# A hybrid encoder layer: gated sums ahead of the bank's sigmoid, first rows of the up half loaded twice, the last norm moved forward, and the down half's first pair made in memory that comes free earlier

## The chip, the cores and the metric

The kernel runs on one core of a Trainium2 chip. The metric is the device time of one execution in microseconds (us). Each time is a median over runs; the profile is of one execution of its own. Engines are named as the profile names them: PE multiplies matrices (PEld loads its weights), DVE is the vector engine, ACT the scalar engine, POOL the general one, SP only starts DMA transfers. Each engine works through its own instructions in order and waits on semaphores for the others.

## The reference

One layer of an encoder, on two sequences of 512 tokens with a model width of 1024, all in float32. The kernel handles the two sequences together (`s` = 0 and 1).

```python
h = rms_norm(x, ln1)
proj = h @ w_in
q, k, v, u, g_att, g_ssm = jnp.split(proj, IN_SPLITS, axis=-1)
...
y_att = windowed_attention(q, k, v, sink, bias, band_mask(seq_len))
y_ssm = s5_branch(u, ...)          # gelu(y) * sigmoid(gelu(y) @ w_glu + b_glu)
mixed = jax.nn.sigmoid(g_att) * y_att + jax.nn.sigmoid(g_ssm) * y_ssm
x = x + mixed @ w_out
h2 = rms_norm(x, ln2)
return x + jnp.square(jax.nn.relu(h2 @ w_up)) @ w_down
```

The inner width of the last line, the squared-ReLU MLP, is 4096.

## The kernel before, in words

Precision is kept by splitting each float32 operand into a high part (a cast to fp32r, on ACT) and a low part (the operand less the high part, a subtract on DVE). One product of two split tiles is three matmuls (`mm3`): high by high (L115), high by low (L116), low by high (L117). So wherever new operands are made, PE waits for a cast on ACT first and for a subtract on DVE second. Order on each engine is set by a scheduler that follows the program's order and its dependencies; where tiles share memory, a later tile waits until the earlier one's last reader is done.

The parts of the program that matter here, in order of time:

**Attention's last division (around 690 to 715 us).** `Divide.invert` makes `rsum` on DVE (L1106); `Divide.turn` transposes it on PE (L1111), copies it to `row` on ACT, sends it to DRAM (`rs_scr<-row`) and fetches it back spread out (`fac`), the DMAs on POOL's queue; `Divide.multiply` multiplies by it on POOL (L1124). Beside that PE computes `ahead`, the first column of the GLU product (`Column.multiply`, L758), in pieces of so many matmuls.

**The GLU (about 700 to 775).** For each column m = 1 to 7 and each sequence s: 24 matmuls into a bank, then `bank_out` (a sigmoid on ACT, L1415, tile `gl`), then `late()`, which is the `mix` of the bank before: two DVE instructions (L1421, L1422, tile `z`), a cast (L1424) and a subtract (L1425) that write the split result into `mixT[s]`. For s = 0 `gate_in` adds a sigmoid of 1024 and two DVE products (L1409 to L1411). The result of column 0 is written by `first_evac` (L1433, L1434). `mixT[0]` lies in `slot_c`, `mixT[1]` in `slot_d`; the tile `row` and others of the attention held memory now under `slot_c`.

**Output projection and second norm (to about 885).** `mixT` times `w_out` plus x, row tile by row tile (class `Rows`): `half` multiplies, `add` and `square` add x and sum the squares, three POOL instructions make `rs`, `norm` makes `rn_xn` (DVE L1524), `turn` transposes it on PE (L1532), and `first_rows`, `old_rows`, `sums_a`, `sums_b` and `sums_c` make the split operands of the MLP.

**The up half (to 1181).** A Strassen-like scheme (Winograd's form): seven products in place of eight on 2 x 2 blocks. One block of `w_up`, r = 0 to 15, gives products p1, p2, p6, p7, p5, p3, p4 in this order, of 12 matmuls each; the right operands B11, B21 (in the memory of `mixT[0]`), T1, B22 (in that of `mixT[1]`), T2, T3, T4 stay. `first_parts` splits the weights of the first two blocks into `f_0` and `f_1` (L1471 cast, L1472 subtract); in `parts` the same is `u_hi` (L1663) and `u_lo` (L1664). Squared-ReLU sums go to DRAM as `a_scr` (tags a22, a21, a12, t1 to t4).

**The down half (from 1181).** `product_d(n)` runs over eight pairs of blocks: it loads `d_a` from `a_scr` (L1797) and `k` from `w_down` (L1800), splits both (L1810 casts, L1811 subtracts: `a_hi`, `a_lo`, `b_hi`, `b_lo`) and makes 24 matmuls into four banks. The order of the seven products is 1, 5, 6, 3, 7, 2, 4.

## Time and profile before

| | us |
|---|---|
| median of 3 runs (lowest, highest) | 1501.79 (1499.71, 1502.31) |
| profiled execution, time | 1500.58 |
| its span | 1498.8 |
| mean granted clock of PE | 0.995 |
| PE busy | 1462.7 (98%) |
| DVE busy | 1095.9 (73%) |
| ACT busy | 764.9 (51%) |
| POOL busy | 168.9 (11%) |

The span is the time between the first and the last instruction of the profiled execution. Matmuls overlap, so one of 512 columns shows 0.39 us though the next starts 0.23 us after it. A row of the timeline has the start, the time, engine, line, operation, the tiles written and read, the count, and in brackets the idle time ahead of it with what ended it.

### The profile page before, as it was taken

Reading aid. Unit: us, or ns where it says so; the run is one execution under the profiler, and the core shown is the slowest. Engines: PE = TensorE matmul, PEld = TensorE weight load, DVE = VectorE, ACT = ScalarE, POOL = GpSimd, SP = SyncE. Lnnn points to the kernel's source line nnn. Section 1 sums busy time; section 2 is a strip of 40 time slices with the busy share of each in tenths; the row PEclk is TensorE's granted clock in tenths of the full one; section 3 lists DMA queues with packets and bytes.
Section 4 is the critical chain, followed back from the end, with each engine's and each line's share of the span. In section 5 each row is a group of like instructions: output and inputs, shape, how many; then the busy total and the mean of one; then the engine's idle time right before and its main releaser. Section 6 shows DMA issues by size and latency. Waiting matters only on the chain.

```text
span 1498.8 us, 22161 instructions
## 1 busy us (share of the span) xinstructions
PE 1462.7 (98%) x8070; PEld 1253.3 (84%) x8070; DVE 1095.9 (73%) x1835; ACT 764.9 (51%) x1366; POOL 168.9 (11%) x270
## 2 busy tenths in 40 slices
PE   6999999999999999999999999999999899999999
PEld 5888888889998888987889978888888688888787
DVE  8799979964637888887874689777776597575653
ACT  6588952234427777786433355555555343433332
POOL 4011120000313333342001000000000000000000
PEclk9999999999999999999999999999999999999999
DMA  8355566459832323147853134444443974454431
GB/s 298 109 174 171 178 218 231 132 181 291 263 101 61 98 65 109 46 149 246 271 198 107 71 121 161 153 148 149 155 155 127 349 268 128 153 183 154 125 121 64
DMA packets 128809, 242.86 MB, mean 162 GB/s; under 512 B 16011, under 2 KB 59275, under 8 KB 128700
## 3 DMA queue, kind: packets, MB, share of 16 engines
q1 hardware_dynamic: 104252, 185.82, 39.1%
q10 hardware_dynamic: 21888, 46.15, 8.1%
q0 software_dynamic: 2560, 9.48, 1.9%
q8 instruction: 64, 1.05, 0.3%
q14 instruction: 45, 0.37, 0.1%
HBM read 172.16 MB, written 81.82 MB: 169 GB/s over the span
## 4 chain that ended last, share of the span: by engine, by line
PE 83%; DVE 7%; ACT 3%; DMA 3%; issue 2%; POOL 1%; SPq 0%; DVEq 0%; ACTq 0%; POOLq 0%
PE bank L116 13%; PE bank L117 13%; PE bank L115 13%; PE acc L146 11%; PE acc L729 7%; PE acc L115 3%; PE acc L117 3%; PE acc L116 3%; PE sps L609 2%; PE po L1085 2%; PE sps L865 2%; PE sps L1053 2%; PE tps L1069 2%; PE lag L624 1%; DVE p L1057 1%
## 5 line engine op out<-in xcount | busy, mean ns | idle before, releaser
L115 PE MATMUL bank<-b_hi,a_hi 128*128 128x512 f32 x448 | 174.2, 392 | 3.9 <-ACT b_hi L1810 3.9
L116 PE MATMUL bank<-b_lo,a_hi 128*128 128x512 f32 x448 | 175.5, 392 | 2.1 <-DVE b_lo L1811 2.0
L117 PE MATMUL bank<-b_hi,a_lo 128*128 128x512 f32 x448 | 175.1, 391 | 0.0
L729 PE MATMUL acc<-w_hi,hT 128*128 128x256 f32 x768 | 165.0, 291 | 0.0
L146 PE MATMUL acc<-hT,c_hi 128*128 128x512 f32 x512 | 161.0, 394 | 0.0
L1810 ACT CAST a_hi<-d_a 128x1024 fp32r<-128x1024 f32 x56 | 59.0, 1054 | 182.0 <-PE bank L116 178.1
L1811 DVE TENSOR_TENSOR a_lo<-d_a,a_hi 128x1024 fp32r<-128x1024 f32 x56 | 68.4, 1223 | 107.1 <-ACT a_hi L1810 105.3
L729 PEld LDWEIGHTS acc<-w_hi,hT 128*128 128x128 f32 x768 | 126.6, 190 | 1.7
L146 PEld LDWEIGHTS acc<-hT,c_hi 128*128 128x128 f32 x512 | 94.6, 188 | 21.0 <-issue 2.5
L729 PE MATMUL acc<-w_lo,hT 128*128 128x256 f32 x384 | 108.2, 282 | 0.0
L115 PEld LDWEIGHTS bank<-b_hi,a_hi 128*128 128x128 f32 x448 | 84.5, 189 | 21.8 <-ACT b_hi L1810 4.3
L116 PEld LDWEIGHTS bank<-b_lo,a_hi 128*128 128x128 f32 x448 | 84.6, 189 | 21.1 <-DVE b_lo L1811 3.7
L146 PE MATMUL acc<-hT,c_lo 128*128 128x512 f32 x256 | 100.2, 392 | 0.0
L115 PE MATMUL bank<-act,u_hi 128*128 128x512 f32 x256 | 99.6, 389 | 0.0
L116 PE MATMUL bank<-act,u_hi 128*128 128x512 f32 x256 | 99.6, 389 | 0.0
L117 PE MATMUL bank<-act,u_lo 128*128 128x512 f32 x256 | 99.6, 389 | 0.0
L117 PEld LDWEIGHTS bank<-b_hi,a_lo 128*128 128x128 f32 x448 | 84.6, 189 | 17.7
L1063 ACT ACTIVATE p<-p,nmx 128x257 f32<-128x257 f32 (+1 forms) x128 | 72.3, 565 | 35.2 <-DVE nmx L1057 34.3
L729 PEld LDWEIGHTS acc<-w_lo,hT 128*128 128x128 f32 x384 | 73.0, 190 | 2.4
L1057 DVE CUSTOM_DVE_ANT_0 p<-sps,bias,nsink 128x256 f32<-128x256 f32 (+1 forms) x128 | 69.2, 541 | 3.2 <-PE acc L1023 0.7
L1663 ACT CAST u_hi<-s 128x512 fp32r<-128x512 f32 x64 | 39.5, 622 | 62.0 <-PE bank L116 45.4
L115 PE MATMUL acc<-w,act 128*128 128x256 f32 (+1 forms) x224 | 68.2, 305 | 1.9 <-ACT act L1424 1.9
(361 smaller groups left out, 3721.2 us busy)
## 6 DMA issues: line engine op xcount, KB each, us to landing
d_a<-a_scr SPq DMA_DIRECT2D x56, 512.0 KB, 3.6
u_raw<-in_w_up_dram SPq DMA_DIRECT2D x32, 512.0 KB, 6.1
a_scr<-t ACTq DMA_DIRECT2D x64, 256.0 KB, 2.1
k<-in_w_down_dram SPq DMA_DIRECT2D x32, 512.0 KB, 5.7
a_scr<-a ACTq DMA_DIRECT2D x48, 256.0 KB, 3.3
c_raw<-in_w_ug_dram SPq DMA_DIRECT2D x44, 256.0 KB, 3.9
ct_scr<-ctab SPq DMA_DIRECT2D x16, 576.0 KB, 3.3
ctab_in<-ct_scr SPq DMA_DIRECT2D x32, 288.0 KB, 4.9
```

The source lines that it names most:

```text
L115: PE.matmul(ps, a[0], b[0], start=first, stop=False)
L116: PE.matmul(ps, a[0], b[1], start=False, stop=False)
L117: PE.matmul(ps, a[1], b[0], start=False, stop=last)
L146: PE.matmul(self.ps[s], self.w[p == 2][:, k, :], hT[s][p == 1][:, k, :], start=i % (3 * KT) == 0, stop=i % (3 * KT) == 3 * KT - 1)
L609: PE.matmul(ps[:, i * P:(i + 1) * P], bm[:, ri, g, :], u_sb[:, g, :], start=True, stop=True)
L729: PE.matmul(ps, act[p == 2][:, k, col:col + P], self.w[k // 4][p == 1][:, k % 4, :], start=i == 0, stop=i == 3 * KT - 1)
L865: PE.matmul(o, ctab[:, ri, gi, 0:T * CH], st[:, ri, g].rearrange("p s k -> p (s k)"), start=False, stop=ri == 1)
L1057: V.tensor_tensor_reduce(self.p[:, h, 1:1 + self.nk], self.s[h][:, 0:self.nk], biases[self.j][h][:, b0:b0 + self.nk], -1.0, nsink[:, hh:hh ...
L1063: S.activation(p, p, AF.Exp, bias=self.nmx[:, h:h + 1], scale=-1.0, accum_out=self.sums[:, h, self.qb:self.qb + 1])
L1663: S.copy(hi, src)
L1810: S.copy(hi, src)
L1811: V.tensor_sub(lo, src, hi.bitcast(F32))
```

## The change

Six things:

A. Ahead of `div.turn()` twelve matmuls of column 1 are issued in place of six.

B. The two slots of `mixT` are swapped: `mixT[0]`, and with it B11 and B21, now lies in `slot_d`, `mixT[1]` in `slot_c`.

C. For the very last bank (m = 7, s = 1) `late()`, the mix of the bank before, is issued ahead of `bank_out`.

D. The rows of `w_up` that p1 and p2 of r = 0 need are loaded a second time, early, into two `w_raw` buffers (`u_raw0`), and split ahead of `rows1[2].sums_a()`.

E. `last.norm()`, the norm of the last row tile, moves ahead of the split of r = 1's rows and of `last.old_rows()`.

F. `entry_parts` loads and splits the first pair of `product_d(1)` (tiles `e_raw`, `e_part`) into `slot_d`, whose last readers are p1 and p2 of r = 15; for r = 15 all split weights are made at the block's start, casts and subtracts of the entry stand behind p7 and u3, and the entry's 24 matmuls (`pair_products`) follow p4 at once. `product_d(1)` skips its first pair; `k1[0]`, which later products read, is loaded behind product 1.

```diff
             div.invert()
-            ahead.multiply(6)
+            ahead.multiply(12)
             div.turn()
...
-    mixT = [slot(slot_c), slot(slot_d)]
+    mixT = [slot(slot_d), slot(slot_c)]
...
-                col.multiply((s + 1) * 3 * KT - col.i)
+                col.multiply(max((s + 1) * 3 * KT - col.i, 0))
...
+                ending = m == KT - 1 and s
+                if ending:
+                    late()
                 gl = bank_out(m, col.ps[s])
-                late()
+                if not ending:
+                    late()
...
             if t == 3:
+                raws0 = [wb0.tile([P, 4, P], F32, tag="w_raw", name="u_raw0", bufs=2) for _ in range(2)]
+                for i, raw in enumerate(raws0):
+                    SP.dma_start(raw, w_up[0, :, i])
                 up_raws = {0: slot_b.tile([P, 4, 4, P], F32, tag="b0", name="u_raw"),
...
             nxt_add()
+            if t == 3:
+                first = [[(homes[r][:, 2 * i], homes[r][:, 2 * i + 1]) for i in range(2)] for r in range(2)]
+                for raw, home in zip(raws0, first[0]):
+                    first_parts(raw, home)()
             old.sums_a()
-        first = [[(homes[r][:, 2 * i], homes[r][:, 2 * i + 1]) for i in range(2)] for r in range(2)]
-        for i in range(2):
-            first_parts(up_raws[0][:, i], first[0][i])()
...
     p2 = product(acc(), first[0][1], B21)
-    last.old_rows()
+    last.norm()
     subs = [first_parts(up_raws[1][:, i], first[1][i]) for i in range(2)]
     for sub in subs:
         sub()
-    last.norm()
+    last.old_rows()
     last.turn()
...
+    def pair_products(ps, hl, r):
+        for rr in range(2):
+            for t in range(4):
+                mm3(ps[t], [q[:, rr, t * P:(t + 1) * P] for q in hl[0]], [q[:, rr, :] for q in hl[1]],
+                    r + rr == 0, r + rr == NPAIR - 1)
...
+        def entry_parts():
+            raw = slot_d.tile([P, 4, 2, HALF], F32, tag="act0", name="e_raw")
+            part = slot_d.tile([P, 4, 2, HALF], F32R, tag="act1", name="e_part")
+            SP.dma_start(raw[:, 0], a_scr[0, :, 0:2, :])
+            SP.dma_start(raw[:, 1], w_down[0, 0, :, 0:2, :])
+
+            def high():
+                for i in range(2):
+                    S.copy(part[:, 2 * i], raw[:, i])
+
+            def low():
+                for i in range(2):
+                    V.tensor_sub(part[:, 2 * i + 1], raw[:, i], part[:, 2 * i].bitcast(F32))
+
+            return high, low, [[part[:, 0], part[:, 1]], [part[:, 2], part[:, 3]]]
...
+            if last_r:
+                w2, w3, w1, w4_, w_a22 = [lambda p=w(): p for w in (w2, w3, w1, w4_, w_a22)]
+                high, low, entry_hl = entry_parts()
+                final = tc.manual_schedule(engines={mybir.EngineType.PE, mybir.EngineType.Activation, mybir.EngineType.DVE})
+                final.__enter__()
             p6 = product(bank(), w2(), T2)
             u2 = combine(V.tensor_add, p6, u1, "u2")
             p7 = product(bank(), w3(), T3)
+            if last_r:
+                high()
             u3 = combine(V.tensor_add, p7, u2, "u3")
+            if last_r:
+                low()
...
-            p4 = product(bank(), raw_parts(raw[:, 3]), T4)
+            p4 = product(bank(), w_a22(), T4)
+            if last_r:
+                entry_ps = [bank() for _ in range(4)]
+                pair_products(entry_ps, entry_hl, 0)
...
-            ps = [bank() for _ in range(4)]
+            ps = entry_ps if n == 1 else [bank() for _ in range(4)]
...
+                if n == 1 and r == 0:
+                    continue
...
         ps = product_d(1)
+        SP.dma_start(k1[0], w_down[0, 0, :, 0:2, :])
```

What the change does to the order on the engines is seen best in excerpts of it. Line numbers after the change are larger: L1111 keeps its number, L1472 becomes L1476, L1476 L1480, L1506 L1510, L1524 L1528, L1545 L1549, L1651 L1659, L1810 and L1811 L1857 and L1858.

PE beside the last division, the difference (`tps<-ident,rsum` is the transpose in `Divide.turn`, the others are matmuls of column 1):

```order
 L758 MATMUL acc<-act_7723,c_hi 128x512
 L758 MATMUL acc<-act_7722,c_lo 128x512
-L1111 MATMUL tps<-ident,rsum 16x128
 L758 MATMUL acc<-act_7724,c_hi 128x512
 L758 MATMUL acc<-b_7725,c_hi 128x512
```

The transpose leaves this place and stands six matmuls further down.

DVE at the end of the second norm, before (`x` is the row tile in `add`, `act` and `t` are split operands, `s` the old rows, `f` the split rows of `w_up`, `a` the sum a11):

```order
L1562 TENSOR_TENSOR tt_9795<-x_9793,tps 128x512
L1472 TENSOR_TENSOR f_9787<-u_raw,f_9787 128x512 x2
L1506 TENSOR_TENSOR x_9676<-acc,x_9676 128x512
L1476 TENSOR_TENSOR act_8773<-tt_9795,act_8772 128x4x128
L1569 TENSOR_TENSOR tt_9796<-tt_9796,s_9741 128x512
L1476 TENSOR_TENSOR t_9393<-tt_9796,t_9393 128x4x128
L1545 TENSOR_TENSOR s_9852<-act_8183,act_8184 128x512
L1545 TENSOR_TENSOR s_9853<-act_8183,act_8184 128x512
L1472 TENSOR_TENSOR f_9788<-u_raw,f_9788 128x512 x2
L1524 SCALAR_TENSOR_TENSOR rn_xn<-x_9676,rs,ln_bc 128x1024
L1651 TENSOR_TENSOR a_9874<-acc,u_9872 128x512
```

and after:

```order
L1566 TENSOR_TENSOR tt_9803<-x_9801,tps 128x512
L1510 TENSOR_TENSOR x_9676<-acc,x_9676 128x512
L1480 TENSOR_TENSOR act_8773<-tt_9803,act_8772 128x4x128
L1573 TENSOR_TENSOR tt_9804<-tt_9804,s_9741 128x512
L1480 TENSOR_TENSOR t_9393<-tt_9804,t_9393 128x4x128
L1528 SCALAR_TENSOR_TENSOR rn_xn<-x_9676,rs,ln_bc 128x1024
L1476 TENSOR_TENSOR f_9792<-u_raw,f_9792 128x512 x2
L1549 TENSOR_TENSOR s_9862<-act_8190,act_8191 128x512
L1549 TENSOR_TENSOR s_9863<-act_8190,act_8191 128x512
L1659 TENSOR_TENSOR a_9878<-acc,u_9876 128x512
```

The first pair of f subtracts is gone from here (it stands seven rows higher, ahead of the sums of `rows1[2]`), and `rn_xn` has moved up past the second pair and the old rows.

ACT at the seam between the up and down halves, before (L1743 and L1744 are the ReLU and the square, `a_scr<-` the DMAs that ACT issues):

```order
L1743 ACTIVATE a_12497<-a_12497 128x512
L1744 ACTIVATE a_12497<-a_12497 128x512
L1810 CAST a_hi<-d_a 128x1024
L1645 DMA a_scr<-a_12497 128x512
L1743 ACTIVATE a_12521<-a_12521 128x512
L1744 ACTIVATE a_12521<-a_12521 128x512
L1810 CAST a_hi<-d_a 128x1024
L1645 DMA a_scr<-t_12525 128x512
L1645 DMA a_scr<-t_12528 128x512
L1743 ACTIVATE a_12551<-a_12551 128x512
L1645 DMA a_scr<-t_12531 128x512
L1744 ACTIVATE a_12551<-a_12551 128x512
```

and after:

```order
L1769 CAST e_part<-e_raw 128x1024 x2
L1857 CAST a_hi<-d_a 128x1024
L1757 ACTIVATE a_12519<-a_12519 128x512
L1758 ACTIVATE a_12519<-a_12519 128x512
L1653 DMA a_scr<-a_12519 128x512
L1757 ACTIVATE a_12539<-a_12539 128x512
L1857 CAST a_hi<-d_a 128x1024
L1758 ACTIVATE a_12539<-a_12539 128x512
L1857 CAST b_hi<-k_1_12621 128x1024
L1857 CAST b_hi<-k_2_12622 128x1024
L1653 DMA a_scr<-t_12543 128x512
```

The entry's two casts stand ahead of the block's first ReLU, and the casts of the next two pairs' `k` ahead of the last. Before, the first cast of `k` (`b_hi<-k_0`) followed the last row shown. On PE the rows behind p4 (`bank<-t,f_hi` and `f_lo`) were those with `b_hi,a_hi`; after, 24 that read `e_part` stand between.

More of the change, by code (lines that the diff above doesn't have):

```diff
@@ L1745, in relu2 @@
             return c
+        def entry_parts():
[10 more added lines that the diff above has]
+            return high, low, [[part[:, 0], part[:, 1]], [part[:, 2], part[:, 3]]]
         for r in range(NPAIR):
+            last_r = r == NPAIR - 1
             raw = up_raws.pop(r) if r in up_raws else up_rows(r)
@@ L1757, in hybrid_layer @@
                 w1, w2, w3, w4_ = [lambda i=i: made[i] for i in range(1, 5)]
+            w_a22 = lambda: raw_parts(raw[:, 3])
+            if last_r:
[3 more added lines that the diff above has]
+                final.__enter__()
             p6 = product(bank(), w2(), T2)
@@ L1777, in hybrid_layer @@
             put_a(3, r, combine(V.tensor_sub, a12, t2, "t4"))
+        final.__exit__(None, None, None)
     up1_cm.__exit__(None, None, None)
@@ L1791, in product_d @@
         def product_d(n):
-            ps = [bank() for _ in range(4)]
+            ps = entry_ps if n == 1 else [bank() for _ in range(4)]
             for r in range(0, NPAIR, 2):
                 rs = slice(r, r + 2)
+                new = {1: (k1, 0, 0), 5: (k2, 0, 1), 6: (k3, 1, 1), 2: (k3, 1, 0)}.get(n)
+                if n == 1 and r == 0:
+                    continue
                 a = d0.tile([P, 2, HALF], F32, tag="d_a", name="d_a", bufs=3)
                 SP.dma_start(a, a_scr[n - 1, :, rs, :])
-                new = {1: (k1, 0, 0), 5: (k2, 0, 1), 6: (k3, 1, 1), 2: (k3, 1, 0)}.get(n)
                 if new:
@@ L1812, in product_d @@
                     hl.append((hi, lo))
-                for rr in range(2):
-                    for t in range(4):
-                        mm3(ps[t], [q[:, rr, t * P:(t + 1) * P] for q in hl[0]], [q[:, rr, :] for q in hl[1]],
-                            r + rr == 0, r + rr == NPAIR - 1)
+                pair_products(ps, hl, r)
             return ps
```

## The prediction

> **What bounds the kernel now.** I read the page first, then PE's waits, then the windows and the timeline at each place that the change touches.
>
> ```profile
> span 1498.8 us, 22161 instructions
> PE 1462.7 (98%) x8070; PEld 1253.3 (84%) x8070; DVE 1095.9 (73%) x1835; ACT 764.9 (51%) x1366; POOL 168.9 (11%) x270
> PE 83%; DVE 7%; ACT 3%; DMA 3%; issue 2%; POOL 1%; SPq 0%; DVEq 0%; ACTq 0%; POOLq 0%
> ```
>
> PE is busy 98% of the span, so time can only come from its holes. From 690 to 1240 us its waits are (engine, tile and line, releaser: us in total, times, longest):
>
> ```profile
> PE bank L115 <- ACT b_hi L1810: 3.9, 1, 3.9
> PE tps L1532 <- DVE rn_xn L1524: 2.1, 1, 2.1
> PE acc L115 <- ACT act L1424: 1.9, 1, 1.9
> PE acc L116 <- DVE w L1392: 0.9, 1, 0.9
> PE tps L1111 <- DVE rsum L1106: 0.9, 1, 0.9
> PE acc L115 <- ACT f L1471: 0.8, 1, 0.8
> ```
>
> Some holes cost more than their length. Windows of 3.41 us (us; PE, PEld, DVE, ACT, POOL busy; granted clock; DMA share, GB/s):
>
> ```profile
> 767.43:770.85 3.41, 2.40 (x18) 1.99 (x17) 3.41 (x4) 0.86 (x2) 0.00 (x0) 1.00 0.00 0
> 770.85:774.26 3.41, 1.40 (x9) 1.20 (x10) 2.66 (x4) 0.62 (x1) 0.00 (x0) 1.00 0.59 174
> 774.26:777.67 3.41, 3.41 (x18) 3.41 (x17) 2.70 (x6) 1.66 (x3) 0.00 (x0) 0.50 1.01 413
> 876.66:880.07 3.41, 1.33 (x11) 0.95 (x10) 3.41 (x6) 0.37 (x1) 0.00 (x0) 1.00 0.00 0
> 880.07:883.48 3.41, 3.41 (x11) 2.64 (x10) 2.48 (x5) 2.74 (x6) 0.00 (x0) 0.50 0.21 77
> ```
>
> A window with PE busy 1.33 or 1.40 us is followed by one at clock 0.50; one with 2.40 is not. So a hole counts once for itself and, from about half a window up, once more for the half-speed window behind it.
>
> Costs are in this form: a 512-wide matmul shows 0.39 us, but the next starts 0.227 us after it (17.90 us for the 81 matmuls of the second row in the last part, less 2 begun ahead of the window), so an idle time x on PE loses x + 0.16.
>
> **The gated sums and the bank's sigmoid (A, B, C).**
>
> ```profile
> 696.04 0.27 PE L1111 MATMUL tps<-ident,rsum 128*16 128x128 f32 x1 [0.90 <-DVE rsum L1106]
> 702.98 1.22 POOL L1119 DMA_DIRECT2D fac<-rs_scr  x2 [5.49 <-DMA rs_scr<-row]
> 702.55 1.29 DVE L1434 TENSOR_TENSOR act<-at,act 128x512 fp32r<-128x512 f32 x2 [3.06 <-ACT gl L1415]
> 711.58 2.61 DVE L1422 TENSOR_TENSOR z<-z,at 128x512 f32<-128x512 f32 x1
> 771.24 0.69 DVE L1422 TENSOR_TENSOR z<-z,at 128x512 f32<-128x512 f32 x1
> 771.96 0.62 ACT L1424 CAST act<-z 128x512 fp32r<-128x512 f32 x1 [3.67 <-DVE z L1422]
> 772.63 0.39 PE L115 MATMUL acc<-w,act 128*128 128x256 f32 x1 [1.88 <-ACT act L1424]
> ```
>
> Six more matmuls of column 1 (6 x 0.227 = 1.4 us) go ahead of the transpose of rsum and fill its 0.90 wait: 1.06 us gained at 696, and the transpose itself starts 0.3 later. But PE stops again at 772.63 for the cast of z of column 7, the end of a chain of DVE and ACT that runs column after column from 702.55. PE only waits there longer, so the 1.06 come back. What counts is the chain's start. L1434 began at 702.55 though the table names an ACT long done; by the program its first half waits for row's memory, so for the landing of rs_scr that lets POOL issue fac at 702.98. With the slots swapped (B) the second half waits instead, and what follows can start 0.3 earlier (half of 1.29 less the 0.3 of the later transpose). The z at 711.58 took 2.61 us against 0.69 at 771.24, beside POOL's product with fac, which now comes 0.3 later and may take the gain back: chain -0.3 to +0.3, I take 0. The sigmoid behind the last cast (C): the cast waits for z until 771.96 with nothing ahead of it on ACT, so there is nothing to gain; gl moves behind it and must be done when DVE takes its next z, about 773.3, which it just is (771.96 + 0.62 + 0.68 = 773.26). But arriving 1.06 earlier, PE is busy only 1.34 us in the window from 767.43, so the next is likely at half speed too; the matmuls left in it from 772.63 are few: 0 to 0.8 us, I take 0.4. Bounds of this part -0.3 to +1.1, taken +0.4.
>
> [...]
>
> **Up half's first rows and the last norm (D, E).**
>
> ```profile
> 870.99 1.29 DVE L1472 TENSOR_TENSOR f<-u_raw,f 128x512 fp32r<-128x512 f32 x2 [1.75 <-ACT f L1471]
> 871.01 0.50 PE L115 MATMUL acc<-act,f 128*128 128x512 f32 x1 [0.82 <-ACT f L1471]
> 877.79 1.28 DVE L1524 SCALAR_TENSOR_TENSOR rn_xn<-x,rs,ln_bc 128x1024 f32<-128x1024 f32 x1
> 879.12 0.66 PE L1532 MATMUL tps<-ident,rn_xn 128*128 128x128 f32 x4 [2.08 <-DVE rn_xn L1524]
> 881.30 0.63 PE L115 MATMUL acc<-act,f 128*128 128x512 f32 x1
> 881.73 0.63 PE L116 MATMUL acc<-act,f 128*128 128x512 f32 x1
> 882.50 0.69 DVE L1555 TENSOR_TENSOR tt<-sps,tt 128x512 f32<-128x512 f32 x1 [0.90 <-ACT x L1551]
> 884.90 0.68 DVE L1664 TENSOR_TENSOR u_lo<-s,u_hi 128x512 fp32r<-128x512 f32 x1
> ```
>
> Two more 256 KB loads go out some 55 us early in front of two x loads on SP; nothing waits at that end, cost 0. The four f instructions (two casts, two subtracts) then run near 865 to 867 while PE still multiplies, so PE's hole of 0.82 + 0.16 = 0.98 closes, and with it 0.4 of slow start, where the first matmuls waited for the two subtracts of 1.29. DVE pays: rows1[2]'s sums come 1.5 us later (two subtracts), which leaves PE alone since those operands are read behind 881. rn_xn, ahead of the two f_1 subtracts and the old rows (1.2 us each), goes from 877.79 to about 873.9; rs, which POOL makes, then sets it. The transposes start when the 24 matmuls of p1 and p2 are done: 871.01 - 0.98 + 24 x 0.227 = 875.5. Gone: 2.08 + 0.16 = 2.24, and the half-speed window, eight matmuls at 0.43 (the rows at 881.30 and 881.73) for 0.23: 1.6. Sum 0.98 + 0.4 + 2.24 + 1.6 = 5.2.
>
> What is late next: DVE is not faster, only reordered. From rn_xn to tt it now also has the f_1 subtracts and the old rows (2.4 us) that stood ahead of rn_xn, and in all it gains only what was taken off it, 1.5 (the two first subtracts, 1.2, and 0.3 of waiting beside them): tt at 882.50 becomes 881.0, u_lo at 884.90 becomes 883.4, done 884.07. PE, after transposes (0.85) and 24 matmuls, is at p6 at 881.8 and at its third matmul, which reads u_lo, at 882.25. So it waits there in two or three pieces, 1.85 us, and at p7's third matmul once more 0.45 (its u_lo is three DVE operations on). Given back: 2.3. Net -2.9. Bounds: -5.2 if p6 does not wait, -1.3 if the pieces let the clock drop (1.6).
>
> **Down half's first pair in the slot freed first (F).**
>
> ```profile
> 1180.80:1204.10 23.30, 18.59 (x72) 14.49 (x71) 16.52 (x17) 7.79 (x9) 0.00 (x0) 0.85 1.03 387
> 1204.10:1222.00 17.90, 17.90 (x81) 14.82 (x80) 14.46 (x14) 7.00 (x8) 0.00 (x0) 1.00 0.91 327
> 1167.49 1.78 SPq L1800 DMA_DIRECT2D k<-in_w_down_dram  x4
> 1183.86 1.03 ACT L1810 CAST b_hi<-k 128x1024 fp32r<-128x1024 f32 x1
> 1184.94 1.22 PE L115 MATMUL bank<-b_hi,a_hi 128*128 128x512 f32 x2 [3.88 <-ACT b_hi L1810]
> L1810 ACT CAST a_hi<-d_a 128x1024 fp32r<-128x1024 f32 x56 | 59.0, 1054 | 182.0 <-PE bank L116 178.1
> L1811 DVE TENSOR_TENSOR a_lo<-d_a,a_hi 128x1024 fp32r<-128x1024 f32 x56 | 68.4, 1223 | 107.1 <-ACT a_hi L1810 105.3
> d_a<-a_scr SPq DMA_DIRECT2D x56, 512.0 KB, 3.6
> k<-in_w_down_dram SPq DMA_DIRECT2D x32, 512.0 KB, 5.7
> ```
>
> In the first window 70 matmuls begin (72 less 2 under way) in 23.30 us; at 0.227 they need 15.9. So the seam between the up and down halves costs 7.4 us, 4.04 of it the wait for b_hi and the rest half speed (mean clock 0.85) and the wait for b_lo. After the change the first pair's operands lie in slot_d, whose last readers are r=15's p1 and p2; k's issues at 1167.49 show when that memory's kind of wait ends. Two loads of 512 KB from 1167.5 land at 1171 to 1173.5; two casts of 1.05 and two subtracts of 1.22 end by 1177, even one after the other; PE ends p4 at 1184.94 - 3.88 - 0.16 = 1180.9. The cover is 3.9 us. 24 matmuls keep PE until 1186.3. In that time pair 1 is made: its a_lo, b_hi and b_lo need memory that p4 frees at 1181.1; a cast (1.05) beside a subtract, four operations of the last block's sums ahead of b_lo on DVE, and b_lo's 1.22 end near 1184.7, 1.6 to 1.9 us early. The relu of a22 stands behind the new casts and is 1.9 later, off PE's path. k1[0] is loaded a second time (512 KB) behind product 1's loads and waits in no one's way until the subtract near 1200. Taken -7.4; bounds 0 (all of it comes back at pair 1) to -7.4.
>
> **Sum.** +0.4 - 2.9 - 7.4 = -9.9. The profiled execution took 1500.58 (span 1498.8); it becomes 1490.7. The median of the runs is 1501.79, so 1491.9 is forecast.
>
> **Rivals.**
> 1. The clock drops after p6's pieces. PE's idle there is 1.9 to 2.2 of a window's 3.41 us if all of it falls into one, so busy 1.2 to 1.5, on the side of the rows with 1.33 and 1.40; over two windows each stays nearer to the 2.40. D and E give 1.3, and the time is 1493.5. Chance 0.20.
> 2. Pair 1 comes late: if b_lo lands behind the last sums of up plus a queue at ACT, PE stands at 1186.3. From 1.9 us later than I have it, each us costs one, and from a hole of 1.7 on a half-speed window 1.6 more: 3 to 4 us given back, 1495 to 1496. For it: today's b_lo waits stand behind just these sums. Against: they now run ahead of it while PE has 5.4 us of work. Chance 0.12.
> 3. All gains hold, p6 included, since ACT and DVE lose their small waits when reordered (the 0.90 before tt at 882.50): up to 2.3 more, 1489.5; with a chain 0.3 shorter 1489. Chance 0.10.
> 4. Slower: the new loads don't leave at 1167.5 but at p4's end, if slot_d's tiles are held by up to the end of the block. Then landing at 1184.7 to 1186.8, casts and subtracts put PE's second operand at 1189: 8 us of hole and two half-speed windows (3.2), 11.2 instead of 7.4, +3.8, and SP holds the other loads of the down half behind it, some 2 us more for pair 1: 1501.8 + 0.4 - 2.9 + 5.8 = 1505. It decides from an issue later than about 1178. Against it: the readers of slot_d end with p2. Chance 0.03.
> 5. The parts don't do what they say (the seam is moved, not closed, with p6's wait and dip): 1499 to 1502. Chance 0.02.
> That short holes leave the clock alone, against the rows at 0.50, would give 1491.5; it has 0.02 of the forecast's case.
>
> **Numbers.** The forecast's case (1490 to 1493) has 0.53. The range from 1488 to 1496 takes in rival 1, rival 3 and most of rival 2. A measurement here tells from 0.2%, 3.0 us: faster 0.95, same 0.02, slower 0.03.
>
> **What would show it.** After: no wait of PE for rsum, f of the first rows, rn_xn or b_hi; the wait for act L1424's successor near 772 longer by about 1 us; a new wait of PE for u_hi and u_lo near 880 of 1.9 us; 24 e_part matmuls from about 1178 without a hole, and the clock at 1.00 across the seam. I am wrong if PE stands before or behind the e_part matmuls, or if p6's wait is above 3 us.

## The result, and the profile after

The changed kernel takes 1492.31 us (median of 4 runs, 1491.97 to 1493.12), the kernel before 1501.28 on the same chip: 9.0 us less, a ratio of 0.9938 with a 95% interval from 0.9925 to 0.9950. The forecast was 1491.9, 9.9 us less. The profiled execution took 1493.12 us, the slowest of the four, so the two profiles differ by 7.5 us only.

The page of the changed kernel, and PE's waits from 690 to 1260 us (us in total, times, longest):

```profile
span 1491.3 us, 22155 instructions
PE 1458.9 (98%) x8070; PEld 1251.9 (84%) x8070; DVE 1096.3 (74%) x1835; ACT 764.2 (51%) x1366; POOL 168.4 (11%) x270
```

```profile
PE acc L115 <- ACT act L1424: 1.9, 1, 1.9
PE acc L116 <- DVE w L1392: 1.7, 1, 1.7
PE bank L115 <- ACT u_hi L1671: 1.1, 1, 1.1
PE bank L116 <- DVE b_lo L1858: 0.7, 1, 0.7
PE po L1085 <- DVE pl L1078: 0.2, 1, 0.2
```

The waits for b_hi (3.9), rn_xn (2.1), rsum (0.9) and f (0.8) are gone. In their place w makes PE wait 1.7 us and not 0.9, and u_hi is new. The 0.7 for b_lo is at product 5 of the down half; before, PE waited 0.8 for one at the seam, where the down half begins.

To see where the time went, both profiles are laid side by side matmul by matmul: PE runs 8070 of them in both, so the n-th matmul marks the same place in the work. Four stretches between such marks (matmuls 4200, 4800, 5550, 6900 and 7050, which start at 667.7, 790.8, 914.3, 1227.9 and 1262.3 us before) hold all that changed; behind the last mark both take 232.4 to 232.5 us:

| stretch | before | after | difference | forecast |
|---|---|---|---|---|
| gated sums, GLU, first output block | 123.06 | 123.85 | +0.79 | +0.4 |
| second norm, first blocks of the up half | 123.58 | 120.95 | -2.63 | -2.9 |
| up half, seam, product 1 of the down half | 313.51 | 306.00 | -7.51 | -7.4 |
| start of product 5 | 34.41 | 34.99 | +0.59 | 0 |
| sum | | | -8.76 | -9.9 |

Ahead of the first mark the profiled execution of the changed kernel had lost 1.0 us, in code that the change doesn't touch. That is why the spans differ by 7.5 and not by 8.8. Over all executions profiled here the first mark stands between 667.3 and 668.7 us; this shift is in every time below, and the stretches are free of it. What differs from execution to execution inside them, such as windows at half speed, they still hold.

The seam, the changed kernel's timeline:

```profile
1170.38 1.05 ACT L1769 CAST e_part<-e_raw 128x1024 fp32r<-128x1024 f32 x1 [1.69 <-DMA e_raw<-a_scr]
1171.62 1.05 ACT L1769 CAST e_part<-e_raw 128x1024 fp32r<-128x1024 f32 x1 [0.19 <-DMA e_raw<-in_w_down_dram]
1172.72 2.35 DVE L1773 TENSOR_TENSOR e_part<-e_raw,e_part 128x1024 fp32r<-128x1024 f32 x2
1182.68 1.22 DVE L1858 TENSOR_TENSOR b_lo<-k,b_hi 128x1024 fp32r<-128x1024 f32 x1
1180.08 0.39 PE L115 MATMUL bank<-e_part 128*128 128x512 f32 x1
1185.52 0.39 PE L115 MATMUL bank<-b_hi,a_hi 128*128 128x512 f32 x1
1185.74 0.39 PE L116 MATMUL bank<-b_lo,a_hi 128*128 128x512 f32 x1
```

The entry's operands are ready at 1175.1, five us before PE begins its 24 matmuls at 1180.08; the second pair's b_lo is done at 1183.9, 1.8 before PE reads it at 1185.74. PE passes without a hole.

The second norm and p6:

```profile
877.26 0.63 PE L1536 MATMUL tps<-ident,rn_xn 128*128 128x128 f32 x4
884.94 0.49 PE L115 MATMUL bank<-act,u_hi 128*128 128x512 f32 x1 [1.13 <-ACT u_hi L1671]
884.27 0.61 ACT L1671 CAST u_hi<-s 128x512 fp32r<-128x512 f32 x1
885.43 0.68 DVE L1672 TENSOR_TENSOR u_lo<-s,u_hi 128x512 fp32r<-128x512 f32 x1
889.35 0.50 PE L117 MATMUL bank<-act,u_lo 128*128 128x512 f32 x1
```

The transposes of rn_xn no longer wait. p6 starts at 884.94, one matmul's time and 1.29 us behind the one before it; its second and third matmuls lose 0.40 and 0.37, p7's third 0.33: 2.4 us.

The windows at column 7 (3.41 us; busy times of PE, PEld, DVE, ACT, POOL; clock; DMA):

```profile
769.56:772.97 3.41, 0.50 (x2) 0.30 (x2) 3.35 (x4) 0.00 (x0) 0.00 (x0) 1.00 0.10 31
772.97:776.39 3.42, 2.74 (x11) 2.52 (x12) 2.49 (x3) 1.31 (x3) 0.00 (x0) 0.50 0.89 268
776.39:779.80 3.41, 3.41 (x18) 3.41 (x17) 2.23 (x4) 1.55 (x3) 0.00 (x0) 0.50 1.02 417
779.80:783.20 3.40, 3.40 (x30) 3.40 (x29) 0.42 (x1) 0.25 (x1) 0.00 (x0) 1.00 0.85 274
```

Two windows run at half speed where there was one.

### The profile page after: what moved, and what is told of

It is laid out like the page before. It is cut to its first block, busy times and chain, and to the rows that moved or that the text cites. A ratio compares the mean times of both kernels' runs of the same rounds, so it can differ in the third digit from the quotient of the medians.

```text
span 1491.3 us, 22155 instructions
## 1 busy us (share of the span) xinstructions
PE 1458.9 (98%) x8070; PEld 1251.9 (84%) x8070; DVE 1096.3 (74%) x1835; ACT 764.2 (51%) x1366; POOL 168.4 (11%) x270
## 4 chain that ended last, share of the span: by engine, by line
PE 81%; DVE 8%; issue 4%; ACT 3%; DMA 2%; POOL 1%; SPq 0%; DVEq 0%; ACTq 0%; POOLq 0%
PE bank L117 13%; PE bank L116 13%; PE bank L115 13%; PE acc L146 11%; PE acc L729 7%; PE acc L115 3%; PE acc L117 3%; PE acc L116 3%; PE sps L609 2%; PE sps L865 2%; PE sps L1053 2%; PE po L1085 2%; PE tps L1069 1%; DVE p L1057 1%; PE lag L624 1%
## 5 line engine op out<-in xcount | busy, mean ns | idle before, releaser
L116 PE MATMUL bank<-b_lo,a_hi 128*128 128x512 f32 x440 | 171.6, 390 | 1.9 <-DVE b_lo L1858 1.9
L117 PE MATMUL bank<-b_hi,a_lo 128*128 128x512 f32 x440 | 171.3, 389 | 0.0
L115 PE MATMUL bank<-b_hi,a_hi 128*128 128x512 f32 x440 | 170.7, 389 | 0.0
L1857 ACT CAST a_hi<-d_a 128x1024 fp32r<-128x1024 f32 x55 | 57.9, 1053 | 180.9 <-PE bank L116 177.7
L1858 DVE TENSOR_TENSOR a_lo<-d_a,a_hi 128x1024 fp32r<-128x1024 f32 x55 | 67.3, 1224 | 101.9 <-ACT a_hi L1857 99.9
```

The costliest lines, as they stand in the source:

```text
L115: PE.matmul(ps, a[0], b[0], start=first, stop=False)
L116: PE.matmul(ps, a[0], b[1], start=False, stop=False)
L117: PE.matmul(ps, a[1], b[0], start=False, stop=last)
L1857: S.copy(hi, src)
L1858: V.tensor_sub(lo, src, hi.bitcast(F32))
```

## The experiments

Each is compared with the kernel before by time, and with the changed kernel by the stretches of its profile. All medians and, each from one profiled execution, the four stretches and the windows at half speed in them:

| run | median us | ratio to before (95%) | gated sums, GLU | norm, p6 | seam | product 5 | windows at half speed |
|---|---|---|---|---|---|---|---|
| before | 1501.28 | | 123.06 | 123.58 | 313.51 | 34.41 | 4 |
| changed | 1492.31 | 0.9938 (0.9925 to 0.9950) | 123.85 | 120.95 | 306.00 | 34.99 | 2 |
| e10, changed again | 1491.25 | 0.9935 (0.9922 to 0.9947) | 122.91 | 120.92 | 306.00 | 35.13 | 1 |
| e1, without A | 1490.83 | 0.9929 (0.9913 to 0.9945) | 120.58 | 120.94 | 306.00 | 34.61 | 0 |
| e2, without E | 1491.79 | 0.9936 (0.9922 to 0.9951) | 123.60 | 120.98 | 306.00 | 34.49 | 2 |
| e3, without D | 1492.44 | 0.9942 (0.9926 to 0.9959) | 123.01 | 122.21 | 306.00 | 34.27 | 1 |
| e4, without F | 1497.22 | 0.9974 (0.9963 to 0.9984) | 123.26 | 120.91 | 311.84 | 34.16 | 3 |
| e5, B alone | 1497.59 | 0.9976 (0.9967 to 0.9985) | 121.69 | 123.63 | 311.89 | 34.94 | 3 |
| e6, p6 first | 1492.55 | 0.9942 (0.9928 to 0.9956) | 123.85 | 122.83 | 306.00 | 35.28 | 3 |
| e11, p6 and p7 first | 1492.15 | 0.9944 (0.9930 to 0.9957) | 122.69 | 121.19 | 306.00 | 35.43 | 1 |
| e12, no last product on POOL | 1490.07 | 0.9930 (0.9917 to 0.9944) | 120.52 | 120.94 | 306.00 | 35.21 | 1 |
| e7, low parts of GLU later | 1489.60 | 0.9921 (0.9906 to 0.9937) | 120.75 | 122.05 | 306.00 | 35.12 | 1 |
| e8, together | 1489.91 | 0.9922 (0.9910 to 0.9935) | 119.12 | 121.50 | 306.00 | 34.03 | 0 |
| e9, together with p7 first | 1487.75 | 0.9914 (0.9900 to 0.9928) | 120.45 | 121.29 | 306.00 | 34.00 | 0 |

Of the variants of the changed kernel only e4 and e9 differ from it by more than 3 us (0.2%); for the others the stretches decide. How far these can be trusted shows where the code is the same: the second repeats to 0.04 us (changed, e10, e1, e4, e12), but the first lies between 122.69 and 123.85 over seven profiles (changed, e10, e2, e3, e4, e6, e11).

**e1: without A.**

```diff
-            ahead.multiply(12)
+            ahead.multiply(6)
             div.turn()
```

> The changed kernel with part A undone: six matmuls of column 1 ahead of the transpose of rsum, as before; B to F stay. My theory: A gains nothing, since PE waits at column 7 for the DVE and ACT chain anyway, and its longer hole there (1.72 us for w in place of 0.93) is what makes two windows at clock 0.50 out of one (0.8 us). So PE's wait for rsum (0.9) returns, the wait for w falls back to 0.7 to 1.0 us, one window at half speed is left, and the stretch up to 790 us is 0.8 us shorter than with the change: 1491.5. Rival: the 0.8 us come from the swapped slots or POOL's product with fac, which stay; then two half-speed windows stay and the time is 1492.3 or more.

PE waits for rsum again, and the stretch is still 3.3 us shorter than the changed kernel's (2.3 against e10). Part of it is as expected: a hole of 1.6 us and no window at half speed. But column 7's z comes 1.45 us earlier too (770.10 against 772.25, less the 0.70 by which this execution was ahead at the first mark), which I had not expected. From this run, DVE and POOL:

```profile
702.82 0.69 DVE L1434 TENSOR_TENSOR act<-at,act 128x512 fp32r<-128x512 f32 x1 [2.49 <-ACT gl L1415]
711.25 0.69 DVE L1422 TENSOR_TENSOR z<-z,at 128x512 f32<-128x512 f32 x1
711.85 2.40 POOL L1124 TENSOR_TENSOR ya<-ya,fac 128x1024 f32<-128x1024 f32 x1 [7.35 <-DMA fac<-rs_scr]
712.63 2.17 DVE L1425 TENSOR_TENSOR act<-z,act 128x512 fp32r<-128x512 f32 x1 [0.69 <-ACT act L1424]
```

and from the changed kernel:

```profile
704.15 0.69 DVE L1434 TENSOR_TENSOR act<-at,act 128x512 fp32r<-128x512 f32 x1 [2.83 <-DMA rs_scr<-row]
712.28 2.39 POOL L1124 TENSOR_TENSOR ya<-ya,fac 128x1024 f32<-128x1024 f32 x1 [6.45 <-DMA fac<-rs_scr]
712.56 2.65 DVE L1422 TENSOR_TENSOR z<-z,at 128x512 f32<-128x512 f32 x1
```

Twice the same thing happens: a DVE instruction that falls beside POOL's product ends half a us after it (715.21 against 714.67; 714.80 against 714.25) instead of taking its 0.69. In e1 the chain is 0.6 us earlier at L1434 (after the 0.70 is taken off), L1422 slips through ahead of POOL, and what is hit is L1425, the last of its group. In the changed kernel's profile it is L1422, and the cast and L1425 behind it are late as well. So between these two profiles the chain is later in two ways, 0.6 us at its start and 0.8 by the collision.

Only part of this belongs to A. e10 is the changed kernel's code once more, and its profile has another split:

```profile
704.57 0.69 DVE L1434 TENSOR_TENSOR act<-at,act 128x512 fp32r<-128x512 f32 x1 [4.19 <-DMA rs_scr<-row]
714.37 2.13 DVE L1425 TENSOR_TENSOR act<-z,act 128x512 fp32r<-128x512 f32 x1 [0.69 <-ACT act L1424]
```

Here L1434 stands 1.7 us later than in e1 (counted from the first mark), since rs_scr took 7.0 us to land and not 5.5; POOL hits L1425 as in e1, and column 7's z is 1.7 us late. What all nine profiles with A and B have (changed, e2, e3, e4, e6, e7, e10, e11, e12) is that the transpose, and with it the issue of rs_scr, is 0.3 to 0.6 us later than in e1. The landing then took 5.5 to 7.0 us, so that L1434 starts at 35.1 to 36.5 us from the first mark, against 34.8 to 35.3 in the four with B and without A (e1, e5, e8, e9). And which instruction POOL hits changes with the execution and not only with A: L1422 in the changed kernel, e2 and e6, L1425 in e10, e4 and e11, L1410 in e3.

**e12: without POOL's last product.**

```diff
-                GP.tensor_tensor(self.ya, self.ya, self.fac, op=ALU.mult)
+                if not self.last:
+                    GP.tensor_tensor(self.ya, self.ya, self.fac, op=ALU.mult)
```

> The changed kernel without POOL's last product with fac (the last two heads' columns of one sequence stay undivided; nothing else is left out). My theory: that product is what makes DVE's z at 712.6 take 2.65 us in place of 0.69, and through the chain it costs column 7's hole the same 1.9 to 2.2 us: the z takes 0.69, PE's waits for w and act at column 7 are together 1.6 to 2.0 us in place of 3.6, and no or one window is at half speed; 1488.5 to 1490.5. Rival: the slow z has another cause (a DMA's traffic): it stays above 2 us, and the waits too.

```profile
711.61 0.69 DVE L1423 TENSOR_TENSOR z<-z,at 128x512 f32<-128x512 f32 x1
PE acc L115 <- ACT act L1425: 1.9, 1, 1.9
```

This kernel leaves two heads' columns of one sequence undivided. The z takes 0.69 us, column 7's z comes 2.2 us earlier (769.34 against 772.25, less the 0.75 of the first mark), the wait for w is gone and the stretch is 3.3 us shorter, one window at half speed with it. POOL's product is the cause, and the chain hands it on in full: 1.96 less at z and 0.2 of an earlier start make the 2.2. In the kernel before z took 2.61 us from 711.58 and POOL's product 2.76 from 710.89, so there too DVE ended 0.54 us behind POOL, as in the changed kernel. What holds DVE until then isn't shown.

**e2: without E.**

```diff
-    last.norm()
+    last.old_rows()
     subs = [first_parts(up_raws[1][:, i], first[1][i]) for i in range(2)]
     for sub in subs:
         sub()
-    last.old_rows()
+    last.norm()
```

> The changed kernel with part E undone: the last norm behind the old rows and the second pair of f subtracts; A to D and F stay. My theory: E only exchanges waits, because DVE does the same work up to u_lo. rn_xn comes 2.4 us later, PE waits 2.0 to 2.4 us for the transposes, and the waits of p6 and p7 (2.4 us together) are gone: p6's third matmul starts within 0.5 us of the changed kernel's 886.2, and the time is 1492.3, plus 1.6 if the hole in one piece brings a window at half speed. Rival: E is worth its whole wait and the window behind it, 2.2 + 1.6: 1496.

```profile
PE tps L1536 <- DVE rn_xn L1528: 2.2, 1, 2.2
874.09:877.51 3.42, 2.29 (x11) 1.56 (x9) 3.27 (x6) 1.64 (x4) 0.16 (x1) 1.00 0.10 38
877.51:880.92 3.41, 2.33 (x15) 2.06 (x16) 3.38 (x5) 1.32 (x3) 0.00 (x0) 1.00 0.00 0
880.92:884.33 3.41, 3.41 (x17) 2.81 (x15) 2.50 (x5) 2.67 (x5) 0.00 (x0) 1.00 0.21 77
```

The wait for rn_xn is back, those of p6 and p7 are gone, and the stretch is the same to 0.03 us. E exchanges one wait for another: a hole of 2.36 us in matmul starts for 2.39 in pieces. And the hole of 2.2 us, as long as the one before, lowered no clock: here a window's end cuts it in two, and both windows are busy for 2.3 us.

**e3: without D.**

```diff
-                raws0 = [wb0.tile([P, 4, P], F32, tag="w_raw", name="u_raw0", bufs=2) for _ in range(2)]
-                for i, raw in enumerate(raws0):
-                    SP.dma_start(raw, w_up[0, :, i])
...
+        first = [[(homes[r][:, 2 * i], homes[r][:, 2 * i + 1]) for i in range(2)] for r in range(2)]
+        for i in range(2):
+            first_parts(up_raws[0][:, i], first[0][i])()
```

> The changed kernel with part D undone: the first rows of the up half loaded once, split behind the last sums as before; A to C, E and F stay. My theory: D is what is worth something, since it takes the two f subtracts (1.2 us) and some waiting out of DVE's stretch that sets u_lo. PE's hole for f returns (0.8 us and a slow start of 0.4) and u_lo of p6 comes 1.2 to 1.5 us later, so the time is 1493.6 to 1493.9. Rival: D only takes away the hole that it closes and p6 takes that back, so without it nothing changes: 1492.3.

The stretch is 1.26 us longer, as expected (1.2 to 1.5), with PE's wait for f of 0.8 and the same waits at p6 and p7. The median shows less, 0.1, and this profile's time even 1.5 less than the changed kernel's: it was 1.4 us ahead at the first mark and lost 0.8 less at column 7, with one window at half speed, and 0.7 less at product 5. The time alone would not have told.

**e4: without F, and e5: B alone.** e4 is the changed kernel with `entry_parts`, the order at r = 15 and `product_d`'s skip taken out; e5 is the kernel before with one line:

```diff
-    mixT = [slot(slot_c), slot(slot_d)]
+    mixT = [slot(slot_d), slot(slot_c)]
```

> The changed kernel with part F undone: the down half's first pair is loaded and split in the down half's own memory, as before; A to E stay. My theory: the seam is worth 7.5 us, of which 0.6 come back at product 5's second b_lo, so the time is 1499.2, with PE's wait for b_hi of 3.9 us and two windows at half speed. Rival: part of the seam only moved behind, to the loads of later pairs; then the difference is 4 us or less, 1496.3 or below.

> The kernel before with part B alone: the two slots of mixT swapped. Undoing F cost only 5.8 us at the seam, where 7.5 had gone. My theory: the other 1.7 are B's, since the memory of B11 and B21 comes free with p2 of the last block, and the loads of the down half's first pairs into it start ahead of the others; so the seam between the halves is 5.6 to 5.9 us long in place of 7.4 (wait for b_hi 1.5, for b_lo 2.5, one window at half speed), and the GLU's chain starts 0.3 to 0.9 us earlier, with the saving at column 7. Time 1497.5 to 1499.5. Rival: the 1.7 come from A to E having shifted the windows of the clock; then the seam stays 7.4 and the time is 1500.5 to 1501.5.

PE's waits at the seam, of e4 and then of e5 (its 3.0 are 2.4 here and one at product 5):

```profile
PE bank L116 <- DVE b_lo L1819: 2.3, 1, 2.3
PE bank L115 <- ACT b_hi L1818: 1.3, 1, 1.3
```

```profile
PE bank L116 <- DVE b_lo L1811: 3.0, 2, 2.4
PE bank L115 <- ACT b_hi L1810: 1.3, 1, 1.3
1171.83 0.33 SPq L1797 DMA_DIRECT2D d_a<-a_scr  x1
1172.20 0.43 SPq L1800 DMA_DIRECT2D k<-in_w_down_dram  x1
```

Without F the stretch is only 5.84 us longer, which lay between my theory (7.5) and the rival (4 or less). e5 has the rest: the swap by itself takes 1.62 us from the seam. Before, four loads of later pairs' k went out first, at 1167.49; after the swap the first pair's two loads stand at the head, at 1171.83 and 1172.20. Of the 1.62, 1.3 are less waiting for b_hi and b_lo (3.99 us in matmul starts against 5.26). So F is worth 5.8 on top of B, and B 1.6; F without B wasn't tried, and `entry_parts` uses the slot that B empties with p2. e5 also shows B at the GLU: 1.4 us less there, with the same single window at half speed. The chain's start gives 0.6 of it (L1434's second half, counted from the first mark). For the rest, as in e1, L1422 slips through ahead of POOL (0.69 us from 711.13, POOL from 711.98), and L1425 is hit (2.42 us from 712.51), which by e10 can differ in another execution.

**e6 and e11: p6's operands first.** In both the last row tile makes T2 and p6's weights ahead of what only p5 and p3 read:

```diff
             V.tensor_sub(self.t1, x12, self.s11)
             V.tensor_sub(self.t2, x22, self.t1)
+            between()
+            put(T2, self.t2, cs)
...
+            put(T1, self.t1, cs)
...
+            put(B22, self.x22, cs)
```

> The changed kernel with the last row tile's sums in another order: the sum T2 and its split, and the split of the weights of p6 (u_hi, u_lo), go ahead of the splits of B22 and T1, which only p5 and p3 read. My theory: PE's new waits at p6 and p7 (2.4 us together) are a matter of DVE's and ACT's order, so they shrink to 0.5 or less: 1490.2 to 1490.5. Rival: DVE is full there and the waits move to p7, p5 and p3: less than 0.7 us gained, 1491.6 or more.

> The changed kernel with only the second order of the last sums (that of e9_all2). My theory: PE's waits at p6 and p7 (2.4 us in the changed kernel, 2.7 and a half-speed window in e6_p6) fall to 0.5 or less; the stretch between 851 and 913 us is 1.9 to 2.2 us shorter than in the changed kernel, 1490.3. Rival: DVE is full, p5 waits instead: less than 0.7 us.

```profile
PE bank L115 <- ACT u_hi L1685: 2.1, 1, 2.1
```

Both missed. In e6 (above) p6 lost 0.5 us only, but p7 waited 2.1 in one piece, with a window at half speed behind it, and the stretch got 1.9 us longer. In e11, with p7's weights ahead too, the loss is 0.46, 0.56 and 0.50 at p6 and p7 and 0.64 at p3: 2.2 us against 2.4, and the stretch is 0.24 longer. The rivals were right: between 874 and 892 us DVE's one wait in e11 is 0.69 us (for the cast of u_hi, at 883.38), and order only decided which product pays.

**e7: the GLU's low parts later.** `mix` returns its subtract, and the next column's subtracts or the gate's products go ahead of it:

```diff
-            V.tensor_sub(lo, z, hi.bitcast(F32))
+            return lambda: V.tensor_sub(lo, z, hi.bitcast(F32))
...
+                if s == 0 and 1 < m < KT - 1:
+                    for sub in subs:
+                        sub()
+                    low()
+                    gate_in(m)
```

> The changed kernel with the GLU's low parts taken one step later: between z and its low part, where DVE waits 0.69 us for ACT's cast, stand the two subtracts of the next column's weights (columns 3 to 6) or the gate's products (column 7). My theory: PE's hole at column 7 is the end of a DVE and ACT chain that is 10.15 us a column against 10.9 us of matmuls, and late from its start. Five waits of 0.69 us less make it 3.4 us shorter, so that the waits for w and act (3.6 us) shrink to 0.5 or less and the half-speed windows go (0.8 to 2.4 us): 1487.0 to 1488.5. Rival: the chain is held by something else (the next column's weights, which now come later and stop PE at a column's start), and the time is 1491.5 or more.

```profile
PE acc L758 <- DVE c_lo L742: 1.0, 1, 1.0
PE acc L115 <- ACT act L1424: 0.4, 1, 0.4
```

Both are right in part: the stretch is 3.1 us shorter, column 7's waits are down to 0.4 and 0.2 and no window there is at half speed; but the weights of column 4 come 1.0 us late. 1489.6 is above the range of my theory. In the profiled execution, which took 1490.26, 1.1 us is a half-speed window behind p6's wait, which the changed kernel did not have in either profile.

**e8 and e9: together.** e8 is e7 without A, with e6's order and with the sum q3 of the down half in four pieces behind product 5's third pair. e9 has e11's order in place of e6's.

```diff
-        V.tensor_add(q3, q1, xq)
-        xq = residual(0, 1)
-        ps = product_d(5)
+        def mid():
+            for t in range(4):
+                V.tensor_add(q3[:, t], q1[:, t], xqs[0][:, t])
+            xqs[0] = residual(0, 1)
+
+        ps = product_d(5, mid)
```

> The changed kernel without A (six matmuls ahead of the transpose), with the order of the last sums of the run before the last, the later low parts of the GLU, and the sum q3 in four pieces behind product 5's third pair in place of one instruction between a_lo and b_lo of its second. My theory: the gains add, except that A undone and the shorter chain work on the same hole: no wait above 1 us on PE between 700 and 1240 except for rsum, no window at half speed: 1484.5 to 1486. Rival: the holes move to the next late operand, and it is no better than the best of the parts: 1487 or more.

> The run e8_all with one more change of order in the last row tile: p7's weights (u_hi, u_lo of the third sum) and T3 go ahead of the splits of T1 and B22, and T3 is made from a buffer of its own, so that it doesn't wait for T1. My theory: the 2.2 us of waiting at p7 in e8_all came from its u_hi standing behind four casts on ACT; with it ahead, p6 and p7 wait 0.5 or less in all, nothing else moves, and the profiled stretch from 700 to 1260 us is 1.7 to 2.2 us shorter than in e8_all: about 2 us faster than it, 1487.0 to 1488.5. Rival: the wait moves on to p5 (T1 and its weights now late) and nothing is gained.

> The changed kernel once more, unaltered, on the same chip as the others of this call, so that they can be compared with it and not only with the kernel before: 1491.5 to 1493; whether one, two or no windows at half speed follow the hole at column 7 depends on where the hole falls in the grid of 3.41 us windows.

e9 is the fastest, 1487.75 against 1491.25 of the changed kernel beside it (1487.33 to 1488.78 against 1489.00 to 1491.64): 3.5 us. e8's median missed its range though its profiled execution, the fastest of the five with 1487.4, has the shortest sum of stretches of all (580.7; e9 581.7): p7 waits 2.0 us in one piece there, as in e6. e9's median is 2.2 us below e8's and in the range that I gave it, but the two ran on different chips and their intervals overlap. The profiles, of e8's fastest execution and e9's slowest, show 0.2 of it in the stretch of p6 and p7. Three of e8's five executions have a granted clock of 0.998 and all of e9's 0.999 or 1.000, so e8's long wait may bring windows at half speed in other executions than the one profiled; that isn't shown. What is left in e9 is the wait for rsum (0.9) and pieces below 0.9.

## Why the prediction was right, point by point

**Total.** -9.0 by the medians, -8.8 by the stretches, -9.9 forecast. The range and the two large terms held; all three terms of the sum were right for reasons that were partly wrong.

**Gated sums and GLU: +0.4 forecast, +0.79 in one profile and -0.15 in the other.** Right: the wait for rsum went and came back at column 7, though at w and not at the cast, where I looked for it; the chain's start did not move (704.76 against 703.76 at L1410, and 1.0 is the first mark's shift); C was worth nothing: e1 has it and e5 has not, and in both the cast starts 0.73 us behind the start of column 7's z. Wrong: that A and B are each about zero. e5 has B at -1.4, and e1 has the changed kernel better by 2.3 to 3.3 without A, of which up to 1.1 can be a half-speed window that e5 had at the same place and e1 had not. They only cancel, and that the term came out near the forecast is luck. The step that failed is A's delay of the chain, 0.3 us on paper: the transpose came 0.3 to 0.6 later than in e1, and the landing of rs_scr, for which the chain then waits, took 5.5 to 7.0 us, a spread that the forecast had at nothing. And I took POOL's collision for a cost that stays, while the DVE instruction that it hits changes from execution to execution.

**D and E: -2.9 forecast, -2.63 measured.** The waits at p6 and p7 were sized 2.3 and measured 2.4. But by the forecast's sum E would keep 1.5 us of its own (2.24 + 1.6 - 2.3), and e2 shows E at 0.0. D is 1.26. The remaining 1.37 is the half-speed window behind rn_xn, which the profile before had and e2's profile, with the same hole, had not: before, PE was busy 1.33 us in one window, in e2 2.29 and 2.33 in the two that the hole fell into. So E may be worth such a window in an execution where the hole falls into one; e2 was profiled once.

**B and F: -7.4 forecast for F, -7.51 measured.** The cover was longer than estimated (5 us for 3.9), the second pair's margin as estimated (1.8). The forecast put all of it to F; 1.6 are B's, which the order of SP's loads would have shown: the price of the swap was looked for at the GLU alone. The sum is right all the same, since the whole cost of the seam was read off the profile before and all of it went.

**Product 5: 0 forecast, +0.59.** The prediction had the new load of k1[0] in no one's way, and it is not what costs here. DVE now has the sum q3 between a_lo and b_lo of product 5's second pair:

```profile
1226.88 2.28 DVE L1877 TENSOR_TENSOR q<-q,xq 128x2048 f32<-128x2048 f32 x1
1229.08 1.22 DVE L1858 TENSOR_TENSOR b_lo<-k,b_hi 128x1024 fp32r<-128x1024 f32 x1
```

Before, it stood ahead of both:

```profile
1233.94 2.28 DVE L1832 TENSOR_TENSOR q<-q,xq 128x2048 f32<-128x2048 f32 x1
1236.14 1.22 DVE L1811 TENSOR_TENSOR a_lo<-d_a,a_hi 128x1024 fp32r<-128x1024 f32 x1
```

The new place comes with the swap: e5, which has neither F nor its load, has it too, and loses 0.53. The place alone costs nothing: e3 and e4 have it and are at 34.27 and 34.16, below before. But in the changed kernel's profile, and in e5's (the second row), DVE had also waited for a load of k a few us ahead:

```profile
1222.33 3.50 DVE L1852 TENSOR_TENSOR k<-k,k 128x1024 f32<-128x1024 f32 x3 [0.75 <-DMA k<-in_w_down_dram]
1228.10 3.50 DVE L1805 TENSOR_TENSOR k<-k,k 128x1024 f32<-128x1024 f32 x3 [0.67 <-DMA k<-in_w_down_dram]
```

The loss follows this wait over the profiles that have the sum there: 34.27 and 34.16 with no such wait (e3, e4), 34.61 with 0.20 (e1), 34.94 with 0.67 (e5), 34.99 with 0.75, 35.13 with 0.84 (e10), 35.28 with 1.03 (e6), 35.43 with 1.14 (e11). And it takes both: e7 and e8 each wait 0.87, and e7 has 35.12, e8, with the sum in pieces further on, 34.03. Why the load is late in some executions and not in others isn't shown.

**The rivals.** None came in the changed kernel's profiles. The clock did not drop at p6, and this was nearer than the forecast had it: there the waits fell into a window with PE busy 2.15 us; in e7, with the same code at p6, much the same waits fell into one with 2.04 us busy (work for 1.23 by the count at the end), and the clock was 0.50 in the next, which is rival 1 (the rows at the end).

## What to carry to other kernels

When one engine is full, moving one of its results ahead can move the wait to the next result: with DVE busy 3.28 of 3.41 us ahead of p6 (878.79 to 882.20 in the changed kernel), E won 0.03 us, e6 and e11 lost 1.88 and 0.24, and D won 1.26, which it took out of the full stretch. A small delay ahead of a long chain can be paid at the chain's end, and a late landing or a collision on the way can make it longer in one execution than in the next (L1434 0.6 us later than in e1 in one profile of the changed kernel, 1.7 in the other), so filling a hole with work that pushes the head of a chain back (A) can cost more than the hole: the stretch is 2.3 and 3.3 us shorter in e1, not all of it by A, for a wait of 0.9. And where a part of a change looks free, look at the other end of what it moves: the swap of two slots was worth 1.6 us at a place 480 us later.

## What the runs showed of the hardware

The granted clock changed on a grid of 3.41 us: before, it was 0.50 from 774.26 to 777.67, from 880.07 to 883.48 and from 1183.86 to 1190.69 us, with 31 and 89 times 3.41 us between the starts, and in the changed kernel from 772.97 to 779.80. The windows of this grid lie differently in each execution (one begins at 767.39 in e12 and at 768.54 in e1, whose first marks are 0.05 us apart), and whether a hole of PE was followed by half speed went with how much work was left in a window. Between 650 and 1240 us in the fourteen profiles, windows at full speed with PE busy 1.41 us or less (15 of them, from 0.50) were each followed by one at 0.50, and those with 2.15 or more by none. Between, both occur. The first two rows are e7's, at p6, then a row each of e12, e8 and e1:

```profile
879.06:882.47 3.41, 2.04 (x7) 0.93 (x6) 3.41 (x6) 1.47 (x3) 0.00 (x0) 1.00 0.00 0
882.47:885.88 3.41, 3.41 (x10) 2.64 (x9) 2.73 (x6) 1.28 (x3) 0.00 (x0) 0.50 0.00 0
767.39:770.80 3.41, 1.53 (x13) 1.29 (x11) 2.69 (x5) 0.73 (x2) 0.00 (x0) 1.00 0.24 56
880.21:883.62 3.41, 1.66 (x8) 1.00 (x6) 2.20 (x4) 1.52 (x3) 0.00 (x0) 1.00 0.00 0
768.54:771.95 3.41, 1.79 (x14) 1.43 (x12) 2.69 (x4) 1.12 (x2) 0.00 (x0) 1.00 0.39 74
```

After e7's and e12's the clock was halved, after e8's and e1's it was not. Busy time overstates the work of scattered matmuls: one alone shows 0.39 us or, in e7's row, up to 0.55, while in a full stretch the next starts after 0.227 (17.90 us for 79 of them before). Counted at 0.227 us for each 512 columns from a matmul's start, e7's window holds work for 1.23 us and e12's for 1.21, e1's for 1.34 and e8's for 1.46. By this count the order comes out right: the 17 windows at full speed followed by one at half speed hold 1.25 or less, and all others at full speed between 650 and 1240 us hold 1.25 or more (the lowest 1.25 and 1.26, then 1.34). So in these profiles the limit lies near five to six such matmuls in a window (1.25 / 0.227 = 5.5). This is an estimate: counted up to a matmul's shown end instead, the two kinds overlap between 1.23 and 1.41, and no run was made for it. Coming back up went with more busy time: windows at half speed with 1.50, 2.33, 2.53, 2.74 and 2.92 us busy were followed by another, those with 3.19 and more by full speed.

A hole of some 2 us therefore cost its length in e2 (2.2 us at rn_xn) and 1.65 more before, where eight matmuls ran at 0.43 us each. Between the two profiled executions of the changed kernel, which are 1.5 us apart, 0.7 is the shift at the first mark and 0.9 lies in the first stretch, with two windows at half speed and one. How the spread of some 3 us among the other executions of a kernel divides isn't shown.
